# Expert stage of a two-layer token mixer: a fixed queue order per engine, weights in 8 KB runs

## The chip, the cores and the metric

The kernel runs on one core of a Trainium2 chip. The metric is the device time of one execution in microseconds (us). The core has TensorE (PE, with its weight loads shown apart as PEld), VectorE (DVE), ScalarE (ACT), GpSimd (POOL), and SyncE (SP), whose queue issues most transfers; the transfers themselves run on the core's 16 DMA engines.

## The reference

The model has two layers. Each layer has token mixers (not touched here) and a mixture of experts over 1280 tokens in layer 0 (1024 latent, 256 context) and 1024 in layer 1. All arithmetic is float32. What the change touches is this part, cut to what matters:

```python
# h: (N, 1024); 32 experts in 4 groups of 8; two experts of one group for each token
eid = grp * 8 + top2(expert logits inside the best group)
# tokens are sorted by expert and cut into blocks of 128; a block belongs to one expert
yb = (silu(xblk @ exp_gate[e]) * (xblk @ exp_up[e])) @ exp_down[e]     # 1024 -> 512 -> 1024
out[token] += yb * gate
```

An expert with more than 128 tokens needs a second block ("overflow").

## The kernel before

**The expert stage.** `experts` (L1479) runs once in each layer: 32 experts, one block of up to 128 tokens each, then a hardware loop over overflow blocks (L1592). The 260 loads of each weight matrix, four to an expert, say that 65 blocks ran: 32 in each layer and one overflow block.

**One expert.** Its tokens' rows are gathered from `hx` by an indirect DMA on POOL's queue (L1507) and transposed on PE, eight 128x128 blocks (`turn`, L1521). Each weight piece of 128x1024 floats is loaded by SP (`load`, L1491, DMA at L1498) and cut (`cut`, L1512) into a high part (a copy rounded to fp32r on ACT, L152) and a low part (source minus high on DVE or POOL, L153). Every product is three fp32r matmuls: high by high, high by low, low by high. `up` (L1535) does a quarter of the gate and up products, 12 matmuls of 512 columns from two pieces, so four calls make 48; `act` (L1544) does the sigmoid on ACT and two multiplications on DVE; `down` (L1550) transposes the result (four blocks), cuts it, and does 24 matmuls from four pieces; ACT copies the sums out (L1565) and POOL scatters them to `yb` by indirect DMA (L1566). So an expert has 12 weight pieces, 72 matmuls and 12 transposes. POOL makes the low part of pieces 3 and 9, and of the first eight pieces of the layer's first expert (`x.head`); DVE makes the rest.

**Runs of memory.** The weights lie as in the reference. A gate or up piece is read in runs of 2 KB, a down piece in runs of 4 KB; every load is 512 KB.

**Buffers.** 14 loaded pieces (`ld`, NL), 16 halves, so eight cut pieces (`hl`, NH), nine work tiles (`wk`), three gathered blocks (`xg`). One load is asked for with each cut, and it takes the buffer that is free longest. In PSUM: `pR` and `pU` (gate and up sums) and `pA` (down sums) twice, `pm` and `pl` (transposes, routing) once.

**What sets the order.** The program's order is only a proposal: the framework plans a timeline of all engines and puts each engine's instructions in the order in which that plan starts them. So products of two experts, transposes and cuts interleave as the plan found best. Semaphores keep the data dependencies. SP issues its loads in its own order and waits, for each, until its buffer is free.

**Routing.** Ahead of the stage, `route` finds each token's experts, and `primary` (L1417) makes the gather and scatter indices. `finish` (L1420) computes the overflow blocks on DVE (some 30 small operations and two for each of the 20 or 16 token columns) with small matmuls into one PSUM tile `pl` (L1472). It is called once, after the third expert.

Of the kernel before, what the change touches and what calls it, by code (L numbers as in the profile page):

```python
# [14 lines left out]
OP = mybir.AluOpType  # L15
# [108 lines left out]
class K:  # L124
# [7 lines left out]

    def ld(self, shape, dt):
        return self.sp.tile(shape, dt, name="ld", bufs=NL)
# [12 lines left out]
    def xg(self):  # L147
        return self.sb.tile([P, D], F32, name="xg", bufs=3)

# [1156 lines left out]
    def router(self, last, R):  # L1306
# [113 lines left out]
        def finish():  # L1420

            t0 = 2 if last else 0
            m = NT - t0
            ct = pp.tile([P, 32], F32, name="pl")
            nc.tensor.matmul(ct, self.ones, S, start=True, stop=True)
            cnt = tl([32], "cnt")
            V.tensor_copy(cnt, ct)
            thr = tl([9], "thr")
# [20 lines left out]
            pid = pp.tile([P, NOV], F32, name="pl")  # L1449
            for c in range(2):  # L1450
# [15 lines left out]
                for i in range(m):  # L1466
                    ro = tl([P], "ro", bufs=4)
                    V.tensor_scalar(ro, io, b[:, i], None, op0=OP.is_equal)
                    bo = tl([32], "bo", bufs=4)
                    V.tensor_scalar(bo[:, :NOV], io[:, 0:NOV], o[:, i], self.tid[:, c, t0 + i:t0 + i + 1],  # L1470
                                    op0=OP.is_equal, op1=OP.mult)
                    nc.tensor.matmul(pid, ro, bo[:, :NOV], start=(c == 0 and i == 0), stop=(c == 1 and i == m - 1))  # L1472
            val = tl([NOV], "val")
            V.tensor_copy(val, pid)
# [4 lines left out]
    def experts(self, l, hx, yb, R, finish, xmid, t0):  # L1479
# [6 lines left out]
        PIECES = [("exp_gate", 2), ("exp_up", 2)] * 4 + [("exp_down", 1)] * 4  # L1486

# [3 lines left out]
        def load(x):  # L1491

            e = x.e
            for i, (name, kh) in enumerate(PIECES):
                src = a[name][l, e] if isinstance(e, int) else a[name][l, bass.ds(e, 1)].rearrange("o d f -> (o d) f")
                h = i // 2 if i < 8 else i - 8
                w = self.ld([P, kh, src.shape[1]], F32)
                nc.sync.dma_start(w, src.rearrange("(k q) f -> q k f", q=P)[:, h * kh:(h + 1) * kh, :])  # L1498
                x.ws.append(w)
                yield  # L1500

        def expert(e, gat, sca, xg, nxt=None):

            x = Expert()
            x.e, x.xg, x.sca, x.nxt, x.ws, x.head = e, xg, sca, nxt, [], False
            x.load = load(x)
# [5 lines left out]
        def cut(x, i):  # L1512

            w = x.ws[i]
            hi, lo = (self.hl(list(w.shape), F32R) for _ in range(2))
            self.split(hi, lo, w, nc.gpsimd if i in (3, 9) or x.head and i < 8 else None)
            if x.nxt is not None:
                next(x.nxt.load)
            return hi, lo

        def turn(x):  # L1521

            x.xT = [self.wk([P, KD, P], F32R) for _ in range(2)]
            for k4 in range(2):
                pt = pp.tile([P, 4, P], F32, name=("pm", "pl")[k4])
                for k in range(4):
                    kk = k4 * 4 + k
                    nc.tensor.transpose(pt[:, k, :], x.xg[:, kk * P:(kk + 1) * P], self.ident)
                self.split(x.xT[0][:, k4 * 4:k4 * 4 + 4], x.xT[1][:, k4 * 4:k4 * 4 + 4], pt)
            x.g = self.scp.tile([P, 512], F32, name="pR", bufs=2)  # L1530
            x.u = self.scp.tile([P, 512], F32, name="pU", bufs=2)
# [3 lines left out]
        def up(x, h):  # L1535
            gw, uw = cut(x, 2 * h), cut(x, 2 * h + 1)
# [12 lines left out]

        def down(x):  # L1550
            pt = pp.tile([P, 4, P], F32, name="pm")
            for f in range(4):
                nc.tensor.transpose(pt[:, f, :], x.s[:, f * P:(f + 1) * P], self.ident)
            h = self.wk([P, 2, 4, P], F32R)
            self.split(h[:, 0], h[:, 1], pt)
            y = [pp.tile([P, 512], F32, name="pA", bufs=2) for _ in range(2)]
            for f in range(4):
                dw = cut(x, 8 + f)
                for i, (hi_, wi) in enumerate(PASS):
                    for n in range(2):  # L1560
                        nc.tensor.matmul(y[n], h[:, hi_, f, :], dw[wi][:, 0, n * 512:(n + 1) * 512],  # L1561
                                         start=(f == 0 and i == 0), stop=(f == 3 and i == 2))
            o = self.wk([P, D], F32)
            for n in range(2):
                nc.scalar.activation(o[:, n * 512:(n + 1) * 512], y[n], AF.Copy)  # L1565
# [6 lines left out]
        x = slot(0)  # L1572
        for _ in x.load:
            pass
        x.nxt, x.head = slot(1), True
        turn(x)
        up(x, 0)
        for e in range(NE):
            for h in range(1, 4):
                up(x, h)  # L1580
            act(x)
            if x.nxt is not None:
                turn(x.nxt)
                x.nxt.nxt = slot(e + 2) if e + 2 < NE else None
# [256 lines left out]
```

## Time and profile before

| | |
|---|---|
| median of three runs | 3727.9 us (3718.53 to 3746.77) |
| the profiled execution, its own time | 3736.02 us |
| its span, first to last instruction | 3734.2 us |
| PE busy, share of the span | 3124.1 us, 84% |
| DVE busy | 2330.9 us, 62% |
| ACT busy | 1869.2 us, 50% |
| POOL busy | 1363.2 us, 37% |
| moved by DMA | 922.44 MB, mean 247 GB/s |
| mean granted TensorE clock | 0.894 |

The shares are means over stages with different limits. The expert stages are about 1162 to 1862 us (layer 0; its overflow block follows) and 2990 to 3673 us (layer 1). A busy PE counts the latency of pipelined matmuls, so a stretch in which PE starts work late can still look busy.

### The profile page before, as it was taken

The page shows a single profiled execution, that of the slowest core. Times are in us where ns is not written, and L with a number is a line of the kernel's source. Part 1 is how long each engine was busy: PE and PEld are TensorE (multiplying, and loading weights), DVE is VectorE, ACT ScalarE, POOL GpSimd, SP SyncE. Part 2 cuts the span into 40 slices and gives each one's busy share as a digit, 9 for nine tenths or more (in the row PEclk, how much of TensorE's full clock was granted, in tenths as well). Part 3 has the DMA queues.
Part 4 walks back from the last instruction along what each step waited for, and adds up shares of the span by engine and source line. Part 5 has one row for each costly group of instructions (what it writes and reads, how often), then busy time and mean ns, then how long its engine had stood idle before and what let it go on. Part 6 is the DMA issues. An engine that isn't in the chain of part 4 may idle for free. (4 is left out here: it accounts for less than half of the span.)

```text
span 3734.2 us, 60191 instructions
## 1 busy us (share of the span) xinstructions
PE 3124.1 (84%) x22308; PEld 2454.6 (66%) x22308; DVE 2330.9 (62%) x3378; ACT 1869.2 (50%) x2773; POOL 1363.2 (37%) x1183
## 2 busy tenths in 40 slices
PE   6998887988996899999638988778888689999982
PEld 3776666776785677777526766656767567777761
DVE  4275564224577877788673565662236877788886
ACT  4344333335335677767553434324353367777763
POOL 0037775112213333343331276743112333333333
PEclk8998888989997899999868988878889899999996
DMA  6587898789638899999756678899794578999985
GB/s 242 193 187 172 174 193 210 213 259 302 224 129 284 274 333 334 338 322 340 274 209 226 169 164 182 187 184 261 238 296 155 200 264 303 336 335 328 334 319 195
DMA packets 830788, 922.44 MB, mean 247 GB/s; under 512 B 341314, under 2 KB 567499, under 8 KB 830492
## 3 DMA queue, kind: packets, MB, share of 16 engines
q1 hardware_dynamic: 792176, 871.07, 76.0%
q0 software_dynamic: 38304, 47.49, 3.8%
q8 instruction: 177, 2.90, 0.3%
q14 instruction: 119, 0.97, 0.1%
q10 hardware_dynamic: 12, 0.00, 0.0%
HBM read 726.92 MB, written 203.23 MB: 249 GB/s over the span
## 5 line engine op out<-in xcount | busy, mean ns | idle before, releaser
L153 DVE TENSOR_TENSOR hl<-ld,hl 128x1024 fp32r<-128x1024 f32 x652 | 893.0, 1409 | 214.6 <-ACT hl L152 207.1
L152 ACT ACTIVATE hl<-ld 128x1024 fp32r<-128x1024 f32 x796 | 812.0, 1059 | 220.6 <-PE pR L1541 144.4
L153 POOL TENSOR_TENSOR hl<-ld,hl 128x1024 fp32r<-128x1024 f32 x144 | 372.7, 2593 | 722.4 <-ACT hl L152 694.4
L1541 PE MATMUL pR<-hl,wk 128*128 128x512 f32 x1560 | 470.9, 411 | 24.9 <-ACT wk L152 9.7
L1541 PE MATMUL pU<-hl,wk 128*128 128x512 f32 x1560 | 460.1, 404 | 1.5 <-ACT hl L152 0.8
L1561 PE MATMUL pA<-hl,wk 128*128 128x512 f32 x1560 | 405.3, 409 | 44.4 <-DVE wk L153 22.6
L374 PE MATMUL pb<-hh,wh 128*128 128x512 f32 (+1 forms) x1000 | 394.4, 396 | 5.8 <-ACT v L407 1.3
L374 PE MATMUL pb<-hl,wh 128*128 128x512 f32 (+1 forms) x1000 | 389.1, 390 | 0.0
L374 PE MATMUL pb<-hh,wl 128*128 128x512 f32 (+1 forms) x1000 | 386.9, 387 | 1.2 <-issue 1.2
L1561 PEld LDWEIGHTS pA<-hl,wk 128*128 128x128 f32 x1560 | 298.9, 195 | 126.0 <-DVE wk L153 30.1
L1541 PEld LDWEIGHTS pR<-hl,wk 128*128 128x128 f32 x1560 | 296.8, 194 | 105.5 <-DVE wk L153 18.7
L1541 PEld LDWEIGHTS pU<-hl,wk 128*128 128x128 f32 x1560 | 297.2, 193 | 72.5 <-DVE hl L153 5.2
L374 PEld LDWEIGHTS pb<-hh,wh 128*128 128x128 f32 x1000 | 200.3, 200 | 73.0 <-issue 13.6
L1253 PE MATMUL pA<-hl,wk 128*128 128x512 f32 x864 | 226.1, 412 | 6.0 <-ACT wk L152 6.0
L374 PEld LDWEIGHTS pb<-hl,wh 128*128 128x128 f32 x1000 | 201.4, 201 | 38.2 <-issue 10.3
L374 PEld LDWEIGHTS pb<-hh,wl 128*128 128x128 f32 x1000 | 200.4, 200 | 35.2 <-issue 4.2
L1077 POOL DMA_DIRECT2D yD<-yt x72 | 58.0, 805 | 420.3 <-ACT yt L1076 385.6
L1253 PEld LDWEIGHTS pA<-hl,wk 128*128 128x128 f32 x864 | 162.3, 195 | 46.7 <-ACT wk L152 6.6
L1065 DVE TENSOR_TENSOR tm<-pR,ST 128x256 f32<-128x256 f32 x76 | 32.1, 423 | 251.5 <-PE pR L1060 239.5
L584 POOL TENSOR_TENSOR gt<-gt,tmp 120x30 f32<-120x30 f32 (+14 forms) x240 | 171.4, 714 | 17.8
L538 PE MATMUL ps<-ar,bk 64*128 64x128 f32 x1280 | 123.2, 331 | 49.1 <-DVE X L543 20.1
L582 POOL TENSOR_TENSOR tmp<-gt 120x30 f32<-120x30 f32 (+14 forms) x240 | 156.6, 652 | 17.3
(424 smaller groups left out, 5316.8 us busy)
## 6 DMA issues: line engine op xcount, KB each, us to landing
ld<-in_exp_gate SPq DMA_DIRECT2D x260, 512.0 KB
ld<-in_exp_up SPq DMA_DIRECT2D x260, 512.0 KB
ld<-in_exp_down SPq DMA_DIRECT2D x260, 512.0 KB
st<-rlD SPq DMA_DIRECT2D x80, 512.0 KB
wr<-in_w_in SPq DMA_DIRECT2D x46, 512.0 KB
rlD<-ar SPq DMA_DIRECT2D x64, 320.0 KB
rlD<-X SPq DMA_DIRECT2D x64, 320.0 KB
btD<-bt SPq DMA_DIRECT2D x64, 320.0 KB
```

What stands on the lines that cost most here:

```text
L152: nc.scalar.activation(hi, src, AF.Copy)
L153: (eng or nc.vector).tensor_tensor(lo, src, hi.bitcast(F32), op=OP.subtract)
L374: mm = nc.tensor.matmul(ps[:, :n], w[:, k, :], h[:, k, c0:c0 + n], start=(k == 0 and i == 0), stop=(k == KD - 1 and i == 2))
L538: mm = nc.tensor.matmul(ps[:, e, c], bk[h, c0 + c].rearrange("q s t -> q (s t)"), ar[h, :, c0 + c, :], start=True, stop=True)
L582: eng.tensor_tensor(tv, gt[:, 0:j, j:j + 1].to_broadcast([n, j, w]), gt[:, j:j + 1, j + 1:32].to_broadcast([n, j, w]), op=OP.mult)
L584: eng.tensor_tensor(gt[:, 0:j, j + 1:32], gt[:, 0:j, j + 1:32], tv, op=OP.add)
L1065: nc.vector.tensor_tensor(tm, RS[:, 1], ST[d], op=OP.add)
L1077: nc.gpsimd.dma_start(self.yD[d][:, ch * C:(ch + 1) * C, :], yt.rearrange("q p d -> q (p d)"))
L1253: nc.tensor.matmul(ps, oo[o][:, k, :], w[k][w_][:, fs], start=(k == 0 and q == 0), stop=(k == KD - 1 and q == 2))
L1541: nc.tensor.matmul(o, x.xT[xi][:, kk, :], w[wi][:, k, :], start=(kk == 0 and i == 0), stop=(kk == KD - 1 and i == 2))
L1561: nc.tensor.matmul(y[n], h[:, hi_, f, :], dw[wi][:, 0, n * 512:(n + 1) * 512], start=(f == 0 and i == 0), stop=(f == 3 and i == 2))
```

## The change

- **Order.** A context `in_order` adds, for every engine but SP, an ordering edge from each instruction of the 32 experts to the one before it on the same engine. Inside it the written order is the queue order.
- **The written order.** In iteration e (expert x, next n1, next but one n2), the operations are: copy out and scatter of expert e-1; gather for expert e+3; low and high parts of piece 1 of n1; `up(x,1)`; pieces 8, 9 of x, second half of the transposes of n1; `up(x,2)`; pieces 10, 11; `up(x,3)`; `act(x)`; `up(n1,0)`; pieces 2 and 3 of n1 (3 on POOL); the transposes of x's activations (`turned`, cut in two halves); first half of the transposes of n2; `down(x)`; pieces 4 to 7 of n1; piece 0 of n2.
- **Who cuts.** POOL makes the low part of one piece of an expert (3) and not two, and none early for the first expert; DVE makes the other eleven.
- **Weights.** The host lays gate and up together and down by pairs, so that a load is 1 MB in 128 runs of 8 KB; the buffers are 7 of 1 MB (`ld2`) in place of 14 of 512 KB, in a pool of their own (`lp`), which is released and allocated again ahead of the experts. A buffer is free when both its pieces are cut. An expert has six loads.
- **Routing of the overflow.** `finish` becomes a generator that is stepped twice in each iteration from the third expert on; each step does two token columns, and their small matmuls go to a PSUM tile that is added to a running sum on DVE.
- The overflow loop uses the same functions, in sequence.

```diff
+    def in_order(self):
+        tc = self.tc
+        cur = self.nc.cur_bb
+        traced = cur.bb.instructions
+        first = traced[-1]
+        yield
...
+        for i in traced[start:]:
+            if i.engine == mybir.EngineType.SP:
+                continue
+            if i.engine in before:
+                tc.add_manual_dep(i, before[i.engine], mybir.DependencyInfo(mybir.DependencyClass.NoSync,
+                                                                            mybir.DependencyReason.DATA), reason="in_order")
+            before[i.engine] = i.name
...
+                for i0 in range(0, m, 2):
...
+                    yield
+                    pid = pp.tile([P, NOV], F32, name="pl")
+                    for i, (ro, bo) in enumerate(rb_):
+                        nc.tensor.matmul(pid, ro, bo[:, :NOV], start=i == 0, stop=i == 1)
+                    V.tensor_tensor(val, val, pid, op=OP.add)
+                    yield
...
-        PIECES = [("exp_gate", 2), ("exp_up", 2)] * 4 + [("exp_down", 1)] * 4
...
+        def load(x, i):
+            e = x.e
+            name, h = ("exp_gu", i) if i < 4 else ("exp_dn", i - 4)
...
+            w = self.ld2()
+            nc.sync.dma_start(w, src)
+            x.w[i] = w.rearrange("q (g k f) -> q g k f", g=2, k=2 if i < 4 else 1)
+
+        def cut(x, *pieces, pool=None):
+            for i in pieces:
+                w = x.w[i // 2][:, i % 2]
+                hi, lo = (self.hl(list(w.shape), F32R) for _ in range(2))
+                self.split(hi, lo, w, nc.gpsimd if i == pool else None)
+                x.cut[i] = hi, lo
...
+        order = [(0, i) for i in range(4)]
         for e in range(NE):
-            for h in range(1, 4):
-                up(x, h)
-            act(x)
-            if x.nxt is not None:
-                turn(x.nxt)
-                x.nxt.nxt = slot(e + 2) if e + 2 < NE else None
-                up(x.nxt, 0)
-            down(x)
-            x = x.nxt
-            if e == 2:
-                finish()
+            order += [(e + 1, 0)] * (e + 1 < NE) + [(e, 4), (e, 5)] + [(e + 1, i) for i in (1, 2, 3)] * (e + 1 < NE)
...
+        late = finish()
+        with self.in_order():
+            for e in range(3):
+                xs[e] = slot(e)
+            for _ in range(NL // 2):
+                ask()
+            x = xs[0]
+            for h in range(3):
+                cut(x, 2 * h, 2 * h + 1)
+                ask()
+            turn(x, 0)
+            turn(x, 1)
+            turn(xs[1], 0)
+            up(x, 0)
+            cut(x, 6, 7)
+            ask()
+            cut(xs[1], 0)
+            for e in range(NE):
+                x, n1, n2 = xs[e], xs.get(e + 1), xs.get(e + 2)
+                if e:
+                    out(xs.pop(e - 1))
+                if e + 3 < NE:
+                    xs[e + 3] = slot(e + 3)
+                if n1:
+                    cut(n1, 1)
+                    ask()
+                if e >= 2:
+                    next(late, None)
+                up(x, 1)
+                cut(x, 8)
+                if n1:
+                    turn(n1, 1)
+                cut(x, 9)
+                ask()
+                up(x, 2)
+                cut(x, 10, 11)
+                ask()
+                up(x, 3)
+                if e >= 2:
+                    next(late, None)
+                act(x)
+                if n1:
+                    up(n1, 0)
+                    cut(n1, 2, 3, pool=3)
+                    ask()
+                turned(x)
+                if n2:
+                    turn(n2, 0)
+                down(x)
+                if n1:
+                    cut(n1, 4, 5)
+                    ask()
+                    cut(n1, 6, 7)
+                    ask()
+                if n2:
+                    cut(n2, 0)
...
         primary()
+        k.lp.release()
+        k.lp = tc.alloc_tile_pool(name="lde", bufs=1, reuse_waits="tile")
```

## Rows read from the trace of the kernel before

**Rows 1.** Windows: us, busy time (x instructions) by engine, PEclk, DMA share, GB/s; three expert stretches.

```profile
1162.00:1862.00 700.00, 623.81 (x2730) 489.29 (x2730) 550.54 (x548) 477.22 (x571) 253.78 (x124) 0.96 0.90 314
1300.00:1750.00 450.00, 415.33 (x1848) 325.80 (x1849) 355.25 (x326) 325.65 (x393) 171.89 (x87) 0.99 0.95 334
2990.00:3673.00 683.00, 615.42 (x2722) 487.87 (x2722) 543.32 (x536) 475.36 (x569) 248.36 (x124) 0.96 0.88 307
```

**Rows 2.** Groups by line, 1300 to 1750: xcount | busy us, mean ns | idle before, releasers.

```profile
L153 DVE TENSOR_TENSOR hl<-ld,hl 128x1024 fp32r<-128x1024 f32 x216 | 291.2, 1388 | 72.8 <-ACT hl L152 72.5
L152 ACT ACTIVATE hl<-ld 128x1024 fp32r<-128x1024 f32 x257 | 263.1, 1061 | 62.5 <-PE pR L1541 44.9 <-PE pA L1561 11.2 <-PE pU L1541 2.0
L1541 PE MATMUL pR<-hl,wk 128*128 128x512 f32 x528 | 158.0, 408 | 9.1 <-DVE wk L153 3.8 <-DVE hl L153 2.3 <-ACT wk L152 2.1
L153 POOL TENSOR_TENSOR hl<-ld,hl 128x1024 fp32r<-128x1024 f32 x43 | 109.9, 2557 | 192.2 <-ACT hl L152 191.8
L153 DVE TENSOR_TENSOR wk<-pm,wk 128x512 fp32r<-128x512 f32 x45 | 30.7, 682 | 15.8 <-ACT wk L152 15.8
```

**Rows 3.** Timeline of PE, 1400 to 1425: start, us, instruction xcount [idle before, releaser].

```profile
1402.32 0.60 PE L1528 MATMUL pm<-ident,xg 128*128 128x128 f32 x4
1416.07 4.83 PE L1561 MATMUL pA<-hl,wk 128*128 128x512 f32 x20
1424.69 0.55 PE L1528 MATMUL pl<-ident,xg 128*128 128x128 f32 x3 [2.19 <-DVE wk L153]
```

**Rows 4.** Waits of PE, first expert stage, 1162 to 1862: total us, times, longest.

```profile
PE pl L1528 <- DVE wk L153: 14.1, 13, 2.2
PE pA L1561 <- DVE wk L153: 10.2, 7, 1.9
PE pl L1472 <- DVE rt_bo L1470: 5.3, 2, 2.7
```

**Rows 5.** Waits of all engines, 1300 to 1750.

```profile
ACT hl L152 <- DMA ld<-in_exp_up: 0.7, 2, 0.3
```

**Rows 6.** Timeline of DVE, then POOL, 1400 to 1425.

```profile
1405.38 0.67 DVE L1548 TENSOR_TENSOR s<-s,pU 128x512 f32<-128x512 f32 x1
1407.84 3.56 DVE L153 TENSOR_TENSOR hl<-ld,hl 128x1024 fp32r<-128x1024 f32 x3 [1.79 <-ACT hl L152]
1418.76 4.67 DVE L153 TENSOR_TENSOR hl<-ld,hl 128x1024 fp32r<-128x1024 f32 x3 [0.98 <-ACT hl L152]
...
1405.17 2.41 POOL L153 TENSOR_TENSOR hl<-ld,hl 128x1024 fp32r<-128x1024 f32 x1
1417.66 2.42 POOL L153 TENSOR_TENSOR hl<-ld,hl 128x1024 fp32r<-128x1024 f32 x1 [10.07 <-ACT hl L152]
```

**Rows 7.** DMA totals: 1144 to 1154, 1900 to 1925, 1300 to 1750 (the last with its slices).

```profile
DMA packets 1863, 3.95 MB, mean 395 GB/s; under 512 B 125, under 2 KB 125, under 8 KB 1863
...
DMA packets 2843, 10.36 MB, mean 414 GB/s; under 512 B 314, under 2 KB 314, under 8 KB 2843
...
GB/s 299 350 372 343 308 324 376 302 320 309 355 330 328 373 348 291 339 350 366 358 333 353 290 345 313 283 323 353 334 338 359 267 323 326 351 369 359 318 365 329
DMA packets 65769, 150.43 MB, mean 334 GB/s; under 512 B 6863, under 2 KB 6863, under 8 KB 65738
```

**Rows 8.** Timeline of DVE, then POOL, before the first expert, 1136 to 1160.

```profile
1136.46 2.26 DVE L1333 TENSOR_TENSOR rt_aeq<-rt_aeq,iob 128x16 f32<-128x16 f32 x1
1145.53 7.05 DVE L1387 TENSOR_TENSOR rt_S<-rt_S,rt_O 128x32 f32<-128x32 f32 x1
...
1143.19 9.34 POOL L153 TENSOR_TENSOR hl<-ld,hl 128x1024 fp32r<-128x1024 f32 x4 [2.21 <-ACT hl L152]
1157.14 1.13 POOL L1507 DMA_INDIRECT xg<-hx,gat  x1 [4.61 <-DVE sca L1415]
```

**Rows 9.** Timeline of ACT, then POOL, end of the first expert stage.

```profile
1846.41 1.09 ACT L1565 ACTIVATE wk<-pA 128x512 f32<-128x512 f32 x2 [4.03 <-PE pA L1561]
...
1860.67 0.97 POOL L1566 DMA_INDIRECT yb<-wk,sca  x1 [7.22 <-DMA yb<-wk,sca]
```

More of the change, by code (lines that the diff above doesn't have):

```diff
@@ L2 @@
 import numpy as np
[L3 removed]
+from contextlib import contextmanager, nullcontext
 import concourse.bass as bass
@@ L148, in xg @@
         return self.sb.tile([P, D], F32, name="xg", bufs=3)
+    @contextmanager
+    def in_order(self):
[4 more added lines that the diff above has]
+        yield
+        assert self.nc.cur_bb is cur
+        start = next(k for k in reversed(range(len(traced))) if traced[k] is first) + 1
+        before = {}
+        for i in traced[start:]:
[5 more added lines that the diff above has]
+            before[i.engine] = i.name
     def split(self, hi, lo, src, eng=None):
@@ L1484, in experts, with expert @@
             nc.gpsimd.memset(xg, 0.0)
[L1486 removed]
         class Expert:
             pass
[L1491 to L1502, printed above, removed]
+        def expert(e, gat, sca, xg):
             x = Expert()
[L1505 to L1506 removed]
+            x.e, x.xg, x.sca, x.w, x.cut = e, xg, sca, {}, {}
             nc.gpsimd.indirect_dma_start(out=xg, out_offset=None, in_=hx,
@@ L1510, in expert @@
             return x
[L1512 to L1516, printed above, removed]
-            if x.nxt is not None:
[L1518 to L1531, printed above, removed]
+        def load(x, i):
+            e = x.e
+            name, h = ("exp_gu", i) if i < 4 else ("exp_dn", i - 4)
+            src = a[name][l, e, h] if isinstance(e, int) else a[name][l, bass.ds(e, 1), h].rearrange("o q f -> (o q) f")
+            w = self.ld2()
+            nc.sync.dma_start(w, src)
+            x.w[i] = w.rearrange("q (g k f) -> q g k f", g=2, k=2 if i < 4 else 1)
@@ new lines, in cut, with turn @@
+        def cut(x, *pieces, pool=None):
[4 more added lines that the diff above has]
+                x.cut[i] = hi, lo
+        def turn(x, k4):
+            if k4 == 0:
+                x.xT = [self.wk([P, KD, P], F32R) for _ in range(2)]
+            pt = pp.tile([P, 4, P], F32, name=("pl", "pm")[k4])
+            for k in range(4):
+                kk = k4 * 4 + k
+                nc.tensor.transpose(pt[:, k, :], x.xg[:, kk * P:(kk + 1) * P], self.ident)
+            self.split(x.xT[0][:, k4 * 4:k4 * 4 + 4], x.xT[1][:, k4 * 4:k4 * 4 + 4], pt)
@@ new lines, in experts, with ask @@
+        for e in range(NE):
+            order += [(e + 1, 0)] * (e + 1 < NE) + [(e, 4), (e, 5)] + [(e + 1, i) for i in (1, 2, 3)] * (e + 1 < NE)
+        asked = iter(order)
+        xs = {}
+        def ask():
+            e, i = next(asked, (None, None))
+            if e is not None:
+                load(xs[e], i)
+        late = finish()
[54 more added lines that the diff above has]
+                    cut(n2, 0)
+            for _ in late:
+                pass
+            out(x)
@@ L1599, in experts @@
             x = expert(ex, ix[0], ix[1], xgs[0])
-            for _ in x.load:
-                pass
-            turn(x)
+            for i in range(6):
+                load(x, i)
+            turn(x, 0)
+            turn(x, 1)
             for h in range(4):
+                cut(x, 2 * h, 2 * h + 1)
                 up(x, h)
             act(x)
+            turned(x)
+            cut(x, 8, 9, 10, 11)
             down(x)
+            out(x)
         return xts
```

68 lines of the change are left out of this document (38 added, 30 removed).

## The prediction, made before the changed kernel was run

> **What bounds the kernel now.** I began with the 40 slices to find the expert stages, then took windows over them [rows 1]. The two stages last 700 and 683 us for 32 experts each: 21.9 and 21.3 us an expert, 37% of the execution. No engine fills them: in the quiet middle PE is busy 92% of the time, DVE 79%, ACT 72%, the DMA engines 95%.
>
> The groups [rows 2] and PE's timeline [rows 3] say what an expert costs. Twenty matmuls take 4.83 us; the last one's latency, 0.41 us by its mean, lies beyond its start, so one starts every (4.83 - 0.41)/19 = 0.233 us, and 72 make 16.8 us. Four transposes take 0.60 us, tail included: 0.15 us each at most, 1.8 us for twelve, and nearer 1.3 us where the next product starts under that tail. PE therefore needs 18.1 to 18.6 us an expert; I take 18.3. The stages hold 32 x 18.3 = 586 us of PE work, so 114 and 97 us are lost. Busy PE overstates itself here: a matmul that starts 0.1 us late is hidden in the latency of the one before.
>
> The waits [rows 4] name the loss: the second half of a block's transposes waits for DVE (2.2 us at a time, also in the timeline, rows 3), down products wait for the low part of their input, the routing matmuls for DVE. On the other side ACT waited for a weight load only 0.7 us in 450 us [rows 5]. So at 95% share the weight stream is close to full, yet is not what anybody waits for: the order is. That decides my forecast.
>
> **The change part by part.** *Period by PE.* I walk one iteration with PE at t = 0 and the products back to back: up(1) to 2.8, half a turn to 3.3, up(2) to 6.1, up(3) to 8.9, up(n1,0) to 11.7, two times four transposes to 12.6, down to 18.3. After up(3), the sigmoid and two DVE products at 0.68 each [the size of the 512-column row in rows 2] take about 2.5 us with their handoffs; the 2.8 us of up(n1,0) lie beside them. The activations' transposes are cut in halves while PE transposes n2; the first low half (half of 0.68 us, behind ACT's half) comes about 0.3 us late for the third pair of down products. Pieces 8 to 11 are cut by 9.8, before 12.6. Pieces 2 to 7 of n1 are cut before the next iteration wants them. A new cut pair waits for the product that frees its buffers: piece 8 for up(1), piece 4 for up(n1,0), piece 6 for the first quarter of down; ACT stands in its queue at each, but always ahead of need. PE would stall 0.3 us: 18.6 us.
>
> *DVE.* Eleven cuts instead of ten. Three in a row take 3.56 us [rows 6], 1.19 each: 13.1 us. With two transposed halves, two products and the split activation halves, 4 x 0.68 + 0.8 = 3.5 us: 16.6 us, under PE. The mean cut in the trace is dearer, 1.39 us [rows 2], and the timeline says why: three cuts take 4.67 us where the first starts while POOL's cut has 1.3 us to go, 1.1 us more than the free three; yet a product read from PSUM runs its 0.67 us fully inside POOL's 2.41 us [rows 6]. A DVE operation on two SBUF tiles is held until POOL is done, one that reads PSUM is not. In the new order POOL's one cut (piece 3) falls beside the transposes' cuts, which read PSUM. So I price the lock at nothing; the cover is those two PSUM operations, and without it the price is a rival below.
>
> *ACT.* Twelve high parts at 1.06, seven halves at no more than 0.6, about 17 us as an upper bound. Hidden.
>
> *Weight stream.* An expert moves 314 GB/s x 700 us / 32 = 6.87 MB [rows 1]. A stretch with 2 KB runs alone reaches 395 GB/s, one with 4 KB runs 414 GB/s [rows 7]. The difference in time per byte is a fixed cost per run; the next doubling gives back half as much, 424 GB/s as my estimate. Two thirds of the weight bytes now go in 2 KB runs, one third in 4 KB: 8 KB runs save 5.5% of the engines' time. In the middle of the stage 334 GB/s fill 95%, 352 GB/s would fill all; less 5.5% that is 371 GB/s, 18.5 us an expert. The bounds: 16.2 us at 424 GB/s, 19.5 us with no gain from longer runs. I take 18.5, as it is from the stage itself.
>
> The price of the Trainium skill would be another: "DMA: Bandwidth & Descriptors", section "Where 436 GB/s comes from", lets the memory side of one core bind a load at about 358 GB/s, which would make 19.2 us an expert. The rows with 395 and 414 GB/s speak against it for one core working alone.
>
> *Together.* PE at 18.6 and DMA at 18.5 will not fit perfectly; I add 0.3 us: **18.9 us an expert**, between 18.3 (PE alone) and 19.3. With 3 us to start and 3 us to end, a stage is 32 x 18.9 + 6 = 611 us: -89 and -72 us.
>
> The stage's end is in this. Now the last copies are done at 1847.5, and the last scatter leaves at 1860.7, having waited for the landing of the one before [rows 9], as several came together. In the new order one scatter leaves per iteration and the last has one before it 12 us earlier; the bounds of its price are 0 and the 7.2 us of that wait, inside my range.
>
> *Ahead of the first expert.* DVE's routing is held by POOL's early cuts: operations of 16 and 32 columns take 2.26 and 7.05 us, the second of them inside POOL's row of four [rows 8], on the way to the first gather. Without those cuts up to 9 us go, but DVE itself then makes eight, 9.5 us, of which some four fit beside the gather's flight. I take -5 us a layer, bounds -9 and +9: **-10 us**.
>
> *Routing in steps.* A layer gets one small addition for each pair of token columns and choice, 10 or 8 in all, and DVE has 2.3 us spare an expert (18.9 less 16.6); the present waits on that PE group, 5.3 us in the first stage [rows 4], are inside the stage's excess already. Bounds 0 and 5; +2 us a layer: **+4 us**. The first step is the largest and delays one iteration.
>
> *Overflow loop.* Two cuts must follow the last load instead of one: 1.2 us, **+1 us**.
>
> The sum: -89 - 72 - 10 + 4 + 1 = -166 us on the profiled execution's 3736.0, so 3570; the median of the runs stands 8.1 us lower, hence **3562 us**.
>
> **The rivals.** *The weight stream paces.* The share stays at 95%, or the longer runs give nothing: 19.5 us an expert either way. For it: the stream is next to full. Against: nobody waits for it today, and single stretches pass 395 GB/s. A stage is 630 us: -70 - 53 - 5 = -128, 3600 us. Chance 0.14.
>
> *POOL's lock strikes.* If DVE comes half a microsecond late, POOL starts piece 3 before DVE has begun piece 2; that cut is then held up to 2.42 us, and the activations' cut stands behind it in the fixed queue, with down waiting: 18.6 + 2.4 = 21.0 us. Stages of 678 us: -22 - 5 - 5 = -32, 3696 us. Chance 0.09. The rule of the Trainium skill, "SBUF — State Buffer", section "SBUF: two separate sides", that whichever of the two starts first keeps the pair of ports for its whole instruction, is what this rival rests on; the rows agree, as the held cut shows.
>
> *Slower: seven buffers starve the stream.* A 1 MB buffer comes free only after both cuts, and some pairs are cut far apart (pieces 0 and 1 of n1 lie on either side of the copies out), so fewer bytes are in flight; then ACT waits for loads, with its whole fixed queue behind. The two stages break even at 21.5 us an expert, 320 GB/s, and lose 1% at 22.1 us, 311 GB/s. At 290 GB/s, among the low slices of today's stream [rows 7], it is 23.7 us: stages of 764 us, +64 + 81 - 5 = +140, 3868 us. Against: about five buffers stay in flight, 5 MB or 14 us of stream. Chance 0.07.
>
> *Nothing changes.* The planned order was as good and the loss is in the handoffs: 3728 us. Against: the 2.2 us waits recur with fixed size. Chance 0.06.
>
> **How the numbers follow.** Main case 0.62, its own range 3511 to 3608 (18.3 to 19.3 us is -38 and +26; the head and the rest -13 and +20); 0.02 for still faster. The range 3515 to 3650 holds the main case and the first rival with room for both going badly together; it leaves out the other three, 0.22. A difference under 1% is what a measurement here cannot tell from none. Faster by over 1%: main, first rival, the fast tail and half of the lock case, 0.83. Within 1%: the other half and no change, 0.10. Slower: 0.07.
>
> **What would show it.** In the trace after: stages of some 611 us; no 2.2 us gap before the second transposes; matmuls 0.233 us apart across up and down; DVE cuts near 1.2 us on the mean instead of 1.39, with eleven an expert; runs of 8 KB in the DMA totals and some 363 GB/s (6.87 MB in 18.9 us) at a share near 1; ACT not waiting for loads. I am wrong if ACT waits for loads by several us an expert, if cuts beside POOL last over 2 us in every iteration, or if DVE routing ahead of the stage ends later than now.

## The result, and the profile after

The changed kernel took **3631.1 us** (median of 4 runs, 3623.64 to 3638.7), the kernel before 3730.3 us beside it (median of 4, 3718.53 to 3746.77): ratio **0.9736, 95% interval 0.9712 to 0.9759**. That is 69 us above the 3562 us predicted, inside the range of 3515 to 3650. The profiled executions are 3736.02 and 3623.64 us, spans 3734.2 and 3621.7 us: the traces differ by 112.5 us, the medians by 99, since the profiled run of after is its fastest and that of before lies 6 us above its median.

The windows of after, over the expert stage of layer 0, its quiet middle and the stage of layer 1 (us, busy time by engine, PEclk, DMA share, GB/s). They answer [rows 1]: 700 and 683 us have become 640 and 630.

```profile
1145.00:1785.00 640.00, 598.67 (x2730) 481.10 (x2730) 536.18 (x627) 483.83 (x603) 168.03 (x91) 0.99 0.91 347
1300.00:1750.00 450.00, 426.50 (x1964) 343.42 (x1963) 385.45 (x441) 351.22 (x439) 125.21 (x69) 1.00 0.94 358
2930.00:3560.00 630.00, 587.95 (x2722) 478.94 (x2722) 532.81 (x615) 482.02 (x603) 189.05 (x92) 0.99 0.89 336
```

The same groups as [rows 2], after, 1300 to 1750 us. DVE's mean cut is 1225 ns (1388 before), POOL makes 23 cuts (43 before), and DVE's and ACT's waits in front of the cuts are 11.0 and 10.2 us (72.8 and 62.5 before).

```profile
L176 DVE TENSOR_TENSOR hl<-ld,hl 128x1024 fp32r<-128x1024 f32 x254 | 300.1, 1225 | 11.0 <-ACT hl L175 5.9 <-PE pR L1571 1.1
L175 ACT ACTIVATE hl<-ld 128x1024 fp32r<-128x1024 f32 x278 | 279.0, 1053 | 10.2 <-PE pR L1571 7.1 <-PE pA L1595 0.3
L1571 PE MATMUL pR<-hl,wk 128*128 128x512 f32 x554 | 161.6, 400 | 0.0
L176 POOL TENSOR_TENSOR hl<-ld,hl 128x1024 fp32r<-128x1024 f32 x23 | 68.0, 2957 | 157.8 <-ACT hl L175 157.8
```

PE's timeline of after (start, us, instruction, idle before and releaser), then its waits over the stage of layer 0 (total us, times, longest). The 2.19 us gap of [rows 3] is gone, as is the wait of `pl` on DVE [rows 4]. In its place one gap stands in **every** iteration, in the middle of the transposes of the activations: the second pair waits 0.93 us for DVE's low cut of the first. The last two rows, of POOL, are two scatters in a row: 19.24 us apart, the period of an expert in layer 0.

```profile
1566.77 0.38 PE L1586 MATMUL pm<-ident,s 128*128 128x128 f32 x2
1568.09 0.44 PE L1586 MATMUL pm<-ident,s 128*128 128x128 f32 x2 [0.93 <-DVE wk L176]
1568.36 0.60 PE L1557 MATMUL pl<-ident,xg 128*128 128x128 f32 x4
1568.72 5.84 PE L1595 MATMUL pA<-hl,wk 128*128 128x512 f32 x24
```

```profile
PE pm L1586 <- DVE wk L176: 32.3, 32, 1.8
...
1556.48 1.50 POOL L1602 DMA_INDIRECT yb<-wk,sca  x1 [6.80 <-ACT wk L1601]
1575.72 1.52 POOL L1602 DMA_INDIRECT yb<-wk,sca  x1 [6.79 <-ACT wk L1601]
```

Ahead of the first expert (after, POOL, then PE): the gather leaves at 1136.07, not at 1157.14 [rows 8] (of these 21 us, 9.4 were gained earlier, in the layer-0 mixers); but PE, whose queue is fixed, waits 1.90 us for the second expert's gather with the first expert's products behind it. At the stage's end the last scatter leaves at 1785.09 and waits for ACT's copy, no longer for the scatter before it [rows 9].

```profile
1136.07 1.93 POOL L1527 DMA_INDIRECT xg<-hx,gat  x1 [33.91 <-DVE sca L1438]
1785.09 0.97 POOL L1602 DMA_INDIRECT yb<-wk,sca  x1 [16.30 <-ACT wk L1601]
...
1145.43 1.11 PE L1557 MATMUL pl<-ident,xg 128*128 128x128 f32 x4 [15.36 <-DMA xg<-hx,gat]
1149.30 1.09 PE L1557 MATMUL pl<-ident,xg 128*128 128x128 f32 x4 [1.90 <-DMA xg<-hx,gat]
```

**Long iterations.** From scatter to scatter an expert takes 19.25 us in layer 0 and 19.0 us in layer 1, but six iterations take 21.6 to 23.5 us: those in which DVE has one of the large steps of `finish` (3.3 to 3.6 us). One of them, after: DVE's cut of piece 2 starts after POOL's cut of piece 3 and is held (1.98 us, not the 1.22 of other iterations); it ends 1.08 us after POOL's; PE waits 1.26 and then 1.73 us, and its 24 down products take 6.84 us, not 5.84. Rows of DVE, POOL and PE:

```profile
1248.44 1.98 DVE L176 TENSOR_TENSOR hl<-ld,hl 128x1024 fp32r<-128x1024 f32 x1
...
1246.14 3.20 POOL L176 TENSOR_TENSOR hl<-ld,hl 128x1024 fp32r<-128x1024 f32 x1 [6.81 <-ACT hl L175]
...
1248.66 0.41 PE L1586 MATMUL pm<-ident,s 128*128 128x128 f32 x2 [1.26 <-DVE s L1578]
1250.80 0.69 PE L1586 MATMUL pm<-ident,s 128*128 128x128 f32 x2 [1.73 <-DVE wk L176]
1252.00 6.84 PE L1595 MATMUL pA<-hl,wk 128*128 128x512 f32 x24
```

**A loss outside the change.** From the last scatter of layer 0 to the last store into `xmid` of layer 1 (combine and layer-1 mixers, whose source is unchanged) the kernel before took 1063.7 us and the kernel after 1084.1, with the same instruction counts on PE and POOL and nearly the same busy time. The first window is of before, the second of after, the third of the experiment `whole`, which differs from after in the expert code alone.

```profile
1890.40:2954.10 1063.70, 864.43 (x7832) 677.51 (x7832) 562.01 (x981) 419.94 (x761) 400.88 (x452) 0.85 0.76 205
```

```profile
1816.20:2900.30 1084.10, 865.05 (x7832) 676.54 (x7832) 552.78 (x980) 418.85 (x761) 401.18 (x452) 0.85 0.75 201
```

```profile
1789.70:2850.50 1060.80, 862.30 (x7832) 672.84 (x7832) 551.05 (x980) 417.76 (x762) 400.83 (x452) 0.86 0.76 206
```

So the span's 112.5 us are: expert parts (last `xmid` store to last scatter, overflow included) 1483.2 to 1359.1, **-124.1**; layer-0 mixers 1125.4 to 1116.0, -9.4; combine and layer-1 mixers **+20.4**; tail +0.7.

### The profile page after: what moved, and what is told of

The parts are those of the page before. It is cut to its first block, busy times and chain, and to the rows that moved or that the text cites. A ratio compares the mean times of both kernels' runs of the same rounds, so it can differ in the third digit from the quotient of the medians.

```text
span 3621.7 us, 59282 instructions
## 1 busy us (share of the span) xinstructions
PE 3063.4 (85%) x22308; PEld 2426.6 (67%) x22308; DVE 2281.6 (63%) x3543; ACT 1880.5 (52%) x2838; POOL 1178.0 (33%) x1101
## 5 line engine op out<-in xcount | busy, mean ns | idle before, releaser
L176 DVE TENSOR_TENSOR hl<-ld,hl 128x1024 fp32r<-128x1024 f32 x734 | 869.2, 1228 | 54.2 <-ACT hl L175 44.2
L175 ACT ACTIVATE hl<-ld 128x1024 fp32r<-128x1024 f32 x796 | 798.5, 1052 | 38.4 <-PE pR L1571 21.9
L1571 PE MATMUL pR<-hl,wk 128*128 128x512 f32 x1560 | 455.1, 400 | 0.0
L1571 PE MATMUL pU<-hl,wk 128*128 128x512 f32 x1560 | 446.9, 395 | 0.0
L397 PE MATMUL pb<-hh,wh 128*128 128x512 f32 (+1 forms) x1000 | 393.0, 394 | 10.2 <-ACT wh L175 5.4
L1595 PE MATMUL pA<-hl,wk 128*128 128x512 f32 x1560 | 382.9, 401 | 0.5 <-ACT wk L175 0.5
L1571 PEld LDWEIGHTS pR<-hl,wk 128*128 128x128 f32 x1560 | 288.3, 189 | 60.7 <-ACT wk L175 0.3
L176 POOL TENSOR_TENSOR hl<-ld,hl 128x1024 fp32r<-128x1024 f32 x62 | 184.2, 2971 | 422.4 <-ACT hl L175 422.4
L1602 POOL DMA_INDIRECT yb<-wk,sca x64 | 94.8, 1482 | 468.2 <-ACT wk L1601 452.1
L1276 PE MATMUL pA<-hl,wk 128*128 128x512 f32 x864 | 226.6, 413 | 7.7 <-POOL wk L176 4.0
L175 ACT ACTIVATE wk<-pm 128x256 fp32r<-128x256 f32 (+1 forms) x195 | 88.8, 455 | 185.6 <-PE pm L1586 169.3
```

The source lines that it names most:

```text
L175: nc.scalar.activation(hi, src, AF.Copy)
L176: (eng or nc.vector).tensor_tensor(lo, src, hi.bitcast(F32), op=OP.subtract)
L397: mm = nc.tensor.matmul(ps[:, :n], w[:, k, :], h[:, k, c0:c0 + n], start=(k == 0 and i == 0), stop=(k == KD - 1 and i == 2))
L1276: nc.tensor.matmul(ps, oo[o][:, k, :], w[k][w_][:, fs], start=(k == 0 and q == 0), stop=(k == KD - 1 and q == 2))
L1571: nc.tensor.matmul(o, x.xT[xi][:, kk, :], w[wi][:, k, :], start=(kk == 0 and i == 0), stop=(kk == KD - 1 and i == 2))
L1595: nc.tensor.matmul(x.y[n], x.h[:, hi_, f, :], dw[wi][:, 0, n * 512:(n + 1) * 512], start=(f == 0 and i == 0), stop=(f == 3 and i == 2))
```

## The experiments

All runs in one table; each ratio is to the runs of before on the same chip. "Expert parts" sums both layers as above; "32 experts" is first to 32nd scatter in layers 0 and 1; the last column is the stretch just described. All are from the traces, in us. The stretch that no run edits falls into two groups, 1055 to 1064 and 1071 to 1085, so whole times mislead by up to 30 us and the two columns before it are the ones to compare. The traces show another order of the queues there: POOL runs its 452 instructions in one and the same order in after, `noorder`, `inter`, `lock` and `steps` (1076 to 1085 us) and in other orders in every other run.

| run | median | ratio to before, 95% interval | expert parts | 32 experts | layer-1 mixers |
|---|---|---|---|---|---|
| before | 3730.3 | | 1483.2 | 660.6, 645.2 | 1063.7 |
| after | 3631.1 | 0.9736 (0.9712-0.9759) | 1359.1 | 609.2, 600.2 | 1084.1 |
| oldruns | 3610.1 | 0.9686 (0.9646-0.9726) | 1358.9 | 609.3, 602.7 | 1063.6 |
| noorder | 3625.7 | 0.9723 (0.9685-0.9761) | 1361.4 | 587.9, 586.4 | 1085.2 |
| oneahead | 3684.7 | 0.9877 (0.9832-0.9923) | 1427.9 | 644.4, 636.0 | 1078.8 |
| oneplan | 3629.4 | 0.9741 (0.9694-0.9788) | 1375.8 | 599.4, 592.7 | 1071.2 |
| whole | 3556.3 | 0.9541 (0.9505-0.9578) | 1314.1 | 585.4, 576.4 | 1060.8 |
| inter | 3556.2 | 0.9546 (0.9508-0.9585) | 1287.6 | 573.0, 564.3 | 1084.9 |
| lock | 3696.5 | 0.9916 (0.9890-0.9941) | 1429.1 | 638.1, 637.9 | 1076.5 |
| steps | 3633.0 | 0.9744 (0.9712-0.9776) | 1358.1 | 605.7, 601.7 | 1082.0 |
| steps2 | 3573.6 | 0.9596 (0.9549-0.9643) | 1342.1 | 598.9, 592.7 | 1054.9 |
| nolock | 3601.1 | 0.9652 (0.9600-0.9704) | 1359.2 | 608.0, 599.3 | 1060.1 |
| combo | 3518.9 | 0.9443 (0.9410-0.9476) | 1280.9 | 567.7, 563.0 | 1056.8 |
| best | 3508.7 | 0.9416 (0.9372-0.9460) | 1268.6 | 564.1, 557.6 | 1057.4 |

**1. The gap between the pairs of transposes.** `whole`:

```diff
-            for f2 in (slice(0, 2), slice(2, 4)):
-                for f in range(f2.start, f2.stop):
-                    nc.tensor.transpose(pt[:, f, :], x.s[:, f * P:(f + 1) * P], self.ident)
-                self.split(x.h[:, 0, f2], x.h[:, 1, f2], pt[:, f2])
+            for f in range(4):
+                nc.tensor.transpose(pt[:, f, :], x.s[:, f * P:(f + 1) * P], self.ident)
+            self.split(x.h[:, 0], x.h[:, 1], pt)
```

> The four activation transposes of an expert are issued together, with one high and one low cut of all four, instead of two pairs that share one PSUM tile. My theory: in the changed kernel PE waits 0.93 us in the row of the second pair of transposes, and 16.8 us over 18 experts, for DVE's low cut of the first pair, since both pairs lie in one tile; without the pairs that wait goes and the period falls by 0.5 to 0.6 us (the one cut is longer than each half, so not all comes back), 32 to 38 us over 64 experts: about 3595 us. Rival: the chain sigmoid, product, transposes, cut sets PE's gap by itself, and one whole cut only ends later: 0 to 0.3 us more per expert, 3631 to 3650 us.

PE, `whole`: the four transposes and the four of n2 follow each other, and the down products wait 0.25 us.

```profile
1563.76 0.60 PE L1585 MATMUL pm<-ident,s 128*128 128x128 f32 x4
1564.19 0.60 PE L1557 MATMUL pl<-ident,xg 128*128 128x128 f32 x4
1565.04 5.86 PE L1594 MATMUL pA<-hl,wk 128*128 128x512 f32 x24 [0.25 <-ACT wk L175]
```

The theory holds: an ordinary iteration is 0.63 us shorter (0.5 to 0.6 were expected), 18.6 and 18.35 us from scatter to scatter. The six long iterations lose 1.3 to 2.9 us each, so that it is 23.8 us in each stage. Of the 75 us in the median another 23 are the layer-1 mixers. Cutting the transposes in halves, meant to let the products start sooner, was a loss. That the second pair waits because both lie in one PSUM tile is argued: no run gave each pair a tile of its own.

`inter` adds cover for what is left (`up` gets a range of its twelve matmuls):

```diff
-                    up(n1, 0)
+                    up(n1, 0, slice(0, 9))
                     cut(n1, 2, 3, pool=3)
                     ask()
                 turned(x)
+                if n1:
+                    up(n1, 0, slice(9, 12))
```

> As the run with one whole cut, and the last three of the twelve matmuls of the next expert's first gate and up half stand behind the activation transposes, so that 3 x 0.235 = 0.7 us of PE's work covers the cuts. My theory (PE paces the expert, and its gap in front of the down matmuls is 0.95 us): all of the gap goes, 0.95 us x 64 = 60 us, about 3570 us. Rival: DVE or the weight stream would pace the expert at 18.8 us or so as soon as PE has no gap: at most 20 us beside the kernel after, 3610 us or more.

The median alone, 3556 us, lies 14 us below the theory's 3570 and yet would say "no better than `whole`". The expert parts say otherwise: 573.0 and 564.3 us, 36 us less than after in each stage, 1.16 us an expert; PE runs 18.1 and 17.85 us an expert without a gap (rows below). Against `whole` the layer-1 mixers took it back (1084.9 against 1060.8). The rival falls: neither DVE nor the weight stream paces at 18.8.

```profile
1557.71 0.60 PE L1584 MATMUL pm<-ident,s 128*128 128x128 f32 x4
1558.07 0.95 PE L1570 MATMUL pU<-hl,wk 128*128 128x512 f32 x3
...
1559.21 5.84 PE L1593 MATMUL pA<-hl,wk 128*128 128x512 f32 x24
```

**2. Weight runs.** `oldruns` keeps the pipeline and lays the weights as before.

```diff
-            nc.sync.dma_start(w, src)
...
+            if i < 4:
+                run("exp_gate", 2 * i, v[:, 0])
+                run("exp_up", 2 * i, v[:, 1])
+            else:
+                run("exp_down", 2 * (i - 4), v[:, :, 0])
```

> The changed kernel's pipeline with the weights as they lay before: runs of 2 KB for gate and up (two transfers of 512 KB into one buffer) and of 4 KB for down. My theory (the order of the queues made the gain and the weight stream has slack at 19.1 us per expert): 0 to 25 us above the kernel after, 3631 to 3656 us. Rival (the gain is the 8 KB runs): the stream falls back to the 414 GB/s at best of the kernel before and the period to its 20.3 us, 3700 us or more.

The medians even fall by 21 us; 20.5 us of that is the layer-1 mixers. The expert parts are equal to 0.2 us: **the 8 KB runs bring no time here.** What they bring is room. DMA totals and window of `oldruns`, then the same of after, 1400 to 1750 us: both move 365 GB/s, at a DMA share (last column but one) of 0.99 with the old runs and 0.95 with the new.

```profile
DMA packets 54511, 127.61 MB, mean 365 GB/s; under 512 B 4869, under 2 KB 4869, under 8 KB 54488
```

```profile
1400.00:1750.00 350.00, 332.29 (x1533) 267.54 (x1531) 297.77 (x323) 274.99 (x344) 98.85 (x54) 1.00 0.99 365
```

```profile
DMA packets 20870, 127.61 MB, mean 365 GB/s; under 512 B 3698, under 2 KB 3698, under 8 KB 6914
```

```profile
1400.00:1750.00 350.00, 333.22 (x1533) 268.09 (x1533) 299.30 (x324) 276.99 (x347) 97.04 (x54) 1.00 0.95 365
```

**3. The order and the look-ahead.** Two edits, alone and together. `noorder` drops the imposed order; `oneahead` keeps it and puts an expert's transposes right in front of its first products; `oneplan` does both.

```diff
-        with self.in_order():
+        with nullcontext():
```

```diff
-            turn(xs[1], 0)
...
-                cut(x, 8)
-                if n1:
-                    turn(n1, 1)
-                cut(x, 9)
+                cut(x, 8, 9)
...
                 if n1:
+                    turn(n1, 0)
+                    turn(n1, 1)
                     up(n1, 0)
...
-                if n2:
-                    turn(n2, 0)
                 down(x)
```

> The same work and the same weight runs, but the fixed queue order of the expert section is not imposed: the planner orders each engine's queue by its own costs. My theory (the hand-made order keeps PE fed): the pairs of transposes and cuts fall late again, 3690 us or more. Rival (the two-experts-ahead transposes and the 8 KB runs do it, whatever the order): within 20 us of the kernel after, 3651 us or less.

> The fixed queue order and the 8 KB runs stay, but the tokens of an expert are transposed one expert ahead, both halves right in front of its first gate and up half, where the kernel before had them in its program. My theory (two experts ahead is what keeps PE fed: the run without the imposed order is as fast as the kernel after): PE waits for sigmoid, two products and the low cut of the first half, some 2.8 us an expert, 180 us in all, about 3810 us. Rival (the order or the weight runs made the gain, and the place of the transposes is worth little): 3660 us or less.

> Transposes one expert ahead and no imposed order: of the change there remain the 8 KB runs, one POOL cut an expert instead of two, the routing in steps and the halves of the activation cut. My theory (the imposed order is worth nothing when the transposes are two ahead, and as little when they are one ahead): as the run one expert ahead in the imposed order, 3670 to 3700 us. Rival (planned and one ahead is what the kernel before is): 3715 us or more.

Three misses. Without the imposed order the kernel is as fast (expert parts 1361.4 against 1359.1): the planner loses 14 and 17 us at the heads of the stages, where its first scatter comes 74 to 76 us after the last `xmid` store instead of 59 to 60, and gains about as much later. Its limit looks like another one, though no run tested it: in 20 us DVE works 18.6, has no idle time between these rows (`noorder`), and three cuts in a row, one of them held by POOL's, take 5.79 us and not 3.5.

```profile
1559.37 2.35 DVE L176 TENSOR_TENSOR hl<-ld,hl 128x1024 fp32r<-128x1024 f32 x2
1561.64 0.42 DVE L176 TENSOR_TENSOR wk<-pm,wk 128x256 fp32r<-128x256 f32 x1
1561.97 5.79 DVE L176 TENSOR_TENSOR hl<-ld,hl 128x1024 fp32r<-128x1024 f32 x3
```

One expert ahead in the fixed order costs 1.0 us an expert (20.3 and 20.0 us), not 2.8: PE (`oneahead`) starts its products without the low part, since two of three need the high part alone. By the pace of other rows (0.36 us for four transposes, 0.233 us a matmul) the first two products start 0.49 us late and the third 0.51 us, 1.0 us together.

```profile
1568.63 0.60 PE L1557 MATMUL pm<-ident,xg 128*128 128x128 f32 x4
1569.48 0.74 PE L1571 MATMUL pR<-hl,wk 128*128 128x512 f32 x2 [0.25 <-ACT wk L175]
1570.46 0.50 PE L1571 MATMUL pR<-hl,wk 128*128 128x512 f32 x1 [0.24 <-DVE wk L176]
```

And one ahead under the planner is as good as after within 17 us of expert parts: **107 of the 124 us come from what `oneplan` still has**, and neither from the order nor from the second expert of look-ahead. By `oldruns`, which kept the imposed order, the runs are out too. What remains is: cuts written well ahead of the products that need them; one POOL cut instead of two, and none early for the first expert; the copies out and the scatter an iteration later; 1 MB buffers; the routing in steps. (The halves of the activation cut remain as well; in the imposed order they were a loss.) The groups of `oneplan`, 1300 to 1750 us, show the waits that went [rows 2]: DVE 29.4 us instead of 72.8 in front of its cuts, ACT 26.0 instead of 62.5.

```profile
L176 DVE TENSOR_TENSOR hl<-ld,hl 128x1024 fp32r<-128x1024 f32 x249 | 319.4, 1316 | 29.4 <-ACT hl L175 25.8 <-PE pR L1571 2.5 <-PE pA L1595 0.7
L175 ACT ACTIVATE hl<-ld 128x1024 fp32r<-128x1024 f32 x271 | 272.5, 1060 | 26.0 <-PE pR L1571 16.1 <-PE pU L1571 5.7 <-PE pA L1595 2.7
```

Which of these it is stays open; no run separates them.

**4. POOL's lock and the long iterations.** `lock` gives POOL piece 2:

```diff
-                    cut(n1, 2, 3, pool=3)
+                    cut(n1, 2, 3, pool=2)
```

> POOL cuts piece 2 of the next expert instead of piece 3; DVE then has the cut of piece 3, two SBUF tiles, next in its fixed queue while POOL works 2.4 us on piece 2, and the activations' low cut stands behind it. My theory (a DVE operation on two SBUF tiles is held until POOL is done; in the kernel after, POOL's cut lies beside operations that read PSUM and costs nothing): the held cut delays the down products by 1.0 to 1.5 us an expert, 64 to 96 us, 3695 to 3727 us. Rival (POOL's cut holds nothing that counts): within 10 us of 3631 us.

The theory holds: 1429.1 against 1359.1 in the expert parts, 70 us or 1.1 us an expert. Rows of `lock`, DVE, POOL and PE: POOL starts first, DVE's cut takes 2.62 us and ends 1.08 us after POOL's, and PE's gap is 1.85 us.

```profile
1568.34 2.62 DVE L176 TENSOR_TENSOR hl<-ld,hl 128x1024 fp32r<-128x1024 f32 x1 [0.41 <-ACT hl L175]
...
1567.50 2.38 POOL L176 TENSOR_TENSOR hl<-ld,hl 128x1024 fp32r<-128x1024 f32 x1 [5.85 <-ACT hl L175]
...
1571.35 0.44 PE L1586 MATMUL pm<-ident,s 128*128 128x128 f32 x2 [1.85 <-DVE wk L176]
```

`steps` splits the setups of `finish` by pairs of `yield` (a pair is one iteration), `steps2` splits them further:

```diff
             c9 = tl([32, 9], "c9")
...
+            yield
+            yield
             ov = tl([32], "ov")
```

> The routing of the overflow rows is cut into finer steps: each setup of some 3.5 us of DVE work between two yields becomes steps of at most about 1 us, five more in all per layer. My theory (in the kernel after, the iterations that last 21.6 to 23.5 us instead of 19.0 to 19.3 are those in which DVE has a large step, about 28 us in the two stages together): those iterations shrink to 20 us or less, 15 to 25 us in all, 3606 to 3616 us. Rival (it is the number of additions and PE handoffs that costs, not the size of a step): 3626 us or more.

> The routing of the overflow rows in still finer steps than the first run with finer steps: no step has more than about 0.8 us of DVE work. There, steps of 0.77 us were free, steps of 1.23 and 1.9 us still made iterations of 22.6 to 23.7 us, in which DVE began its cut of piece 2 after POOL had begun piece 3 and was held for 2.8 to 3.4 us. My theory (a step costs nothing up to about 1 us and 3 us beyond that, by POOL's lock): the 32 experts of a stage, first to last scatter, take 595 and 591 us instead of 606 and 602; the layer-1 mixers are planned as in the runs with 1061 to 1064 us there, so the whole is 3590 us or so. Rival (the additions as such cost it): 604 us or more in both stages.

`steps` missed: nothing in the median, 1 us in the expert parts. The long iterations had only changed place, 22.5 to 23.7 us each. Steps of up to 1.0 us were free, those of 1.6 and 1.7 us were not, and the one of 1.2 us fell on either side: free in layer 0, where DVE's cut started 0.14 us ahead of POOL's (1279.20 and 1279.34), and 4.75 us in layer 1 (rows below), where POOL starts 0.06 us ahead and DVE's cut takes 3.38 us. DVE, then POOL and PE:

```profile
3049.22 0.74 DVE L1477 TENSOR_REDUCE rt_xs<-rt_xq 128x18 f32<-128x576 f32 x1
3056.94 3.38 DVE L176 TENSOR_TENSOR hl<-ld,hl 128x1024 fp32r<-128x1024 f32 x1
...
3056.88 2.36 POOL L176 TENSOR_TENSOR hl<-ld,hl 128x1024 fp32r<-128x1024 f32 x1 [6.60 <-ACT hl L175]
...
3060.70 0.69 PE L1596 MATMUL pm<-ident,s 128*128 128x128 f32 x2 [2.83 <-DVE wk L176]
```

With no step above 0.8 us (`steps2`) no iteration is longer than 19.9 us and the expert parts fall by 17.0 us, where 23 were expected; an iteration with a routing product still takes 0.4 us more (19.7 and 19.4 us). Of the 57 us in the median another 29 are the layer-1 mixers.

`nolock` takes POOL's cut away:

```diff
-                    cut(n1, 2, 3, pool=3)
-                    ask()
+                    cut(n1, 2)
...
                 down(x)
                 if n1:
+                    cut(n1, 3)
+                    ask()
```

> POOL cuts nothing in the expert stages: DVE makes the cut of piece 3 too, behind the down products in program order, so that it has twelve cuts an expert, 1.2 us more. The routing steps are those of the kernel after. My theory (DVE has 2 us spare an expert at 19.1 us; the iterations of 21.6 to 23.5 us come from POOL's lock): the usual period stays at 19.0 to 19.3 us, and the iterations with a large step last 21 us at most; first to last scatter 603 and 594 us or so, 6 us less than after each. Rival (DVE needs POOL's share, or the lock is not the cause): period 19.8 us or more, or the long iterations as before.

The period stays at 19.25 and 19.0 us: POOL's share is worth nothing in this order. But the iterations with a step of 3.5 us still take 21.7 to 22.9 us, so there the lock is not needed. The expectation of 21 us at most missed. PE (`nolock`) waits for DVE's product `s` itself:

```profile
1227.81 0.44 PE L1586 MATMUL pm<-ident,s 128*128 128x128 f32 x2 [2.55 <-DVE s L1578]
1229.28 0.44 PE L1586 MATMUL pm<-ident,s 128*128 128x128 f32 x2 [1.03 <-DVE wk L176]
1229.91 7.38 PE L1595 MATMUL pA<-hl,wk 128*128 128x512 f32 x24
```

The cause of these long iterations is thus DVE's lateness; the lock made the steps of 1.2 (layer 1) to 1.7 us about as dear as those of 3.5. That is read from the traces of `steps`: no run had small steps and no POOL cut.

**5. Together.** `combo` is `inter` and `steps`, with the second expert's first transposes moved behind the first expert's products:

```diff
-            turn(xs[1], 0)
             up(x, 0)
+            turn(xs[1], 0)
```

> Three edits together: one whole activation cut with three matmuls of the next expert moved behind the transposes, the finer routing steps, and the second expert's first transposes behind the first expert's first products. The layer-1 mixers are planned here in the order of the runs that spent 1061 to 1064 us there, not 1084. My theory (each cost is its own): the run with the first edit took 3556 us, of which 24 us go by that order, 15 to 25 us by the finer steps and 4 to 6 us by the transposes: 3501 to 3513 us. Rival (PE is full at 18.1 us, so what DVE saves in its steps is hidden): about 3530 us.

3518.9 us, between the two. Moving the transposes brought nothing: from the last `xmid` store to the first scatter it is 60.2 and 59.0 us, in `inter` 59.3 and 57.8. The steps brought 6.6 us, where 15 to 25 were expected; the mixers 28.

`best` is `inter` with the finest steps.

> One whole activation cut with three matmuls of the next expert moved behind the transposes, and the finest routing steps; the layer-1 mixers as planned in the runs with 1057 to 1064 us there. My theory (PE paces the stage at 17.9 to 18.1 us and only the lock's iterations lie above): five iterations of 19.6 to 19.8 us in the run of three edits fall to 18.5 or less, 8 us, 3508 to 3514 us. Rival (PE is full there too): 3519 us as that run.

**3508.7 us**, ratio 0.9416 (0.9372 to 0.9460), the fastest of all. In 400 us of its stage of layer 0 PE has no idle time, and the stream runs at 383 GB/s with a share of 0.99:

```profile
1300.00:1700.00 400.00, 400.00 (x1880) 326.00 (x1879) 365.00 (x427) 329.55 (x394) 121.14 (x65) 1.00 0.99 383
```

## Why the prediction was right in sign and 69 us short

In span terms it said -166 and the traces show -112.5. By its own steps:

- **Stages, -89 and -72: measured -58.9 and -52.9** (first transposes to last scatter, 639.7 and 628.9 us against 611). This is 49 of the 54 us missing. The two stages are 47 us longer than the 611 us each: some 14 by the period, 19.25 and 19.0 us against 18.9, and most of the rest by the routing (next point). In the period the step that failed is "PE would stall 0.3 us". The walk treated the two halves of the activation cut as independent; both pairs lie in one PSUM tile, and the second pair waits 0.93 us for the reader of the first. `whole` prices the halves at 47.6 us in both stages, the shorter long iterations included. That the period is not further off is luck: PE's work is 18.1 and 17.85 us where there is no gap (`inter`), not 18.3, and the 0.3 us for the misfit of PE and DMA does not exist.
- **Routing in steps, +4: measured about 25**, and it lies inside the stages: 17 us for the long iterations (`steps2`) and some 0.4 us for each of the 18 additions. The step that failed is "The first step is the largest and delays one iteration": there are three large steps a layer, and each costs 2.6 to 4.5 us.
- **DVE and POOL's lock**: cuts at 1.23 us and no price in the ordinary iteration, as said. DVE starts piece 2 at 1565.50 in one such iteration, POOL piece 3 at 1566.10: the cover is a head start of 0.60 us (0.17 where the iteration has an addition). The rival's condition ("If DVE comes half a microsecond late") was exact; it held in three iterations of each layer, so it gave part of those 17 us, not a time of 3696. The Trainium skill, "SBUF — State Buffer", section "SBUF: two separate sides", has the rule that the one that starts first keeps the ports for its whole instruction. The traces agree in both directions: with POOL first, a DVE cut of 1.22 us took 2.62 (`lock`) and 3.38 us (`steps`) and ended 1.08 us after POOL's; with DVE first, POOL's cut took 2.83 us and more, not 2.41 (after).
- **Weight stream, 18.5 us an expert**: too dear. The old runs did 19.25 us at a share of 0.99, the new ones 18.1 us at 0.99 (`best`). The saving by longer runs was priced at 5.5% and is 4% of the share (0.99 to 0.95 at equal GB/s); in after it is worth no time. The price of 19.2 us that the prediction took from the Trainium skill, "DMA: Bandwidth & Descriptors", section "Where 436 GB/s comes from", does not bind one core working alone: 383 GB/s over 400 us.
- **Ahead of the first expert, -10: measured -13.7.** From the last `xmid` store to the first gather -11.7 and -11.2, from there to the first transposes +4.5 and +4.7.
- **Overflow loop, +1: measured +1.4.** Stage end: as said.
- **Not in the sum:** the mixers, -9.4 and +20.4. The prediction took untouched code for untouched time. The planner makes one plan of the whole program, and edits in the expert code moved it: the layer-1 stretch lies between 1055 and 1085 us in runs that share its source, with other queue orders. Which instruction of the mixers decides was not traced.

That the loss is in the order ("the order is") was half right: the waits went, but the imposed order is not what removed them (`noorder`, `oneplan`). What it is good for shows in `whole` to `best`: with the order fixed a recurring gap can be found in the trace and taken out; whether the planner would have gained as much from the same edits was not tried.

Of the rivals, "the weight stream paces" gave the nearest number (3600) for a wrong reason; "seven buffers starve the stream" falls, since no engine of after waits for a weight load between 1300 and 1750 us, and "nothing changes" by the time.

## What to carry to other kernels

When a tile is filled and read in halves to gain time, ask whether the second writer waits for the reader of the first half: the halves cost 0.63 us in an ordinary iteration here, and whole was faster. In a queue of fixed order, the largest step of side work counts, not the sum: steps of up to 1.0 us were free, and one of 1.2 us was free in one layer and as dear as one of 3.5 us in the other. Where a planner orders the whole program, compare by stretches of the trace; a median mixes the edit with a re-plan of code that nobody touched.

## What the runs showed of the hardware

- **TensorE's clock fell after two short stalls.** In the long iteration of after PE worked without a gap, then was idle 1.26 us, ran two transposes, and was idle 1.73 us; the granted clock of the next microseconds was 0.50 (1.2 GHz) and came back to 1.00 (2.4 GHz) some 3 us later. The 24 down products took 6.84 us instead of 5.84. Four windows of after, 1 us each:

```profile
1249.00:1250.00 1.00, 0.07 (x1) 0.00 (x0) 1.00 (x1) 0.38 (x1) 0.33 (x1) 1.00 0.97 401
1251.00:1252.00 1.00, 1.00 (x7) 1.00 (x6) 0.05 (x1) 0.38 (x1) 0.00 (x0) 0.50 1.19 320
1253.00:1254.00 1.00, 1.00 (x4) 0.81 (x3) 0.74 (x2) 1.00 (x2) 0.00 (x0) 0.50 0.97 410
1255.00:1256.00 1.00, 1.00 (x6) 0.82 (x5) 1.00 (x2) 1.00 (x2) 0.00 (x0) 1.00 0.04 16
```

- **Whichever of POOL and DVE comes second pays.** POOL's cut took 2.41 us in [rows 6] when it started first and 2.96 us on the mean in after, where DVE usually starts first; there the loss lies on POOL, which waits 6.8 us for other work before its next scatter (the row of 1575.72 above).
